# New order tables for three engines, the last store on ScalarE's queue, and split or joined small transfers in a two-layer trunk

## The chip, the cores and the metric

The kernel runs on one core of a Trainium2 chip. Its engines are TensorE (PE, matmuls), VectorE (DVE), ScalarE (ACT), GpSimd (POOL) and SyncE (SP, which here only issues transfers). Each works through its own instructions in order and waits for the others by semaphores; transfers (DMAs) are issued from the queues of SP, ACT and POOL and run on 16 DMA engines. The metric is the time of one execution on the device in microseconds (us), the median of several runs.

## What is computed

A trunk of two layers on 256 positions of 1024 columns, in 32-bit floats. Each layer has a token mixer beside a cross-attention into 256 memory tokens, an output projection, a layer norm, a SwiGLU network and another layer norm:

```python
for i in range(2):
    if i == 0:   # mixer A: gated MLP, causal in chunks of 128 positions
        u, v, q_mem = jnp.split(x @ a_w_in, [768, 1536], axis=-1)
        mix = gelu(u) * (tril(w_s) @ layer_norm(gelu(v), ln_v_g, ln_v_b) + b_s)
    else:        # mixer B: causal attention, 12 heads of 64 (256 positions are one block)
        q, k, v, q_mem = jnp.split(x @ b_w_in, [768, 1536, 2304], axis=-1)
        mix = causal_attention(q, k, v)
    sub = jnp.concatenate([mix, memory_cross_attention(q_mem, mem, w_mem_kv[i])], -1) @ w_mix_out[i]
    x = layer_norm(ALPHA * x + sub, ln_mix_g[i], ln_mix_b[i])
    g, h = jnp.split(x @ w_ffn_in[i], 2, axis=-1)
    x = layer_norm(ALPHA * x + (silu(g) * h) @ w_ffn_out[i], ln_ffn_g[i], ln_ffn_b[i])
```

The sums with b_s are over groups of 64 columns, with one bias for each group and position.

## The kernel before

*Splits.* Every operand of a matmul is written as a high part and a low part, and a product is three passes (high-high, high-low, low-high). The high part is a cast on ScalarE (L376), the low part a subtraction on VectorE (L377), both by a helper, so that most of these two engines' work carries those two lines. Names that begin with spl_ are such pairs of a weight; x0T, x1T, x2T and x3T are the pairs of the transposed activations ahead of each projection or FFN.

*Weights.* They lie in main memory as units of 1 MB or less and are loaded ahead by SyncE (L237) into four raw buffers and, for one unit of each FFN group, into one of two buffers (gb, vbig) which also hold vectors of the layer norms. Each unit is split in two halves, _0 and _1, in ten buffers. A raw buffer comes free when VectorE has split its second half; SyncE's next load then goes out. In the FFN, pairs of column blocks (groups s..1, 3, 5, 7, 9) are computed by seven products M1 to M7 of combined blocks in place of eight. The combined weights are formed by additions on VectorE (L255) or by accumulating transfers, which GpSimd issues (L219) as soon as the M1 or M3 half in the same buffer has been split.

*Order.* TensorE runs in the order in which the program is written. For VectorE, ScalarE and SyncE, three tables of numbers (VECTOR_ORDER, SCALAR_ORDER, SYNC_ORDER) say in which order the instructions of each engine stand, by their number in the program; `keep_order` (L354 and after) chains them so. GpSimd has no table.

*Places that matter below.* The start: v's projection (va) from x0T. At 24 to 60 us: SyncE loads memory tokens (mraw), the gate's weights (wsT) and position biases (bs, L928, into the ends of the buffers named wsT and vn), the norm's vectors gv, and the units vm0, o0_0 to o0_3; the memory attention's scores (sm) need key tiles that ScalarE and VectorE write through one pair of buffers (kkm, L639 and L640; klm, L641). At 100 to 146 us the first FFN begins: for each group, products Xf, Yf, Zf in PSUM are added up in m1f, m5f and u2f; m5f times the sigmoid sgf (L801) is transposed by TensorE (tpf, L822) for the FFN's second matrix. At 262 to 285 us the FFN's norm: residual with the mixer norm's gain and offset (gain_rows, L531 and L532), statistics (L483, L489), L491 adds the epsilon, GpSimd takes the power -1/2 (L492), then L495 (minus mean, times gain) and L496 (times the power, plus offset), and TensorE transposes the result (ptb). At 300 to 355 us the second mixer's scores (s) from qks, at 372 to 395 us the second FFN's start (x3T, m1g, transposes ptc). At the end the last norm works on pieces of 512, 384 and 128 columns and stores each (L498).

## Time and profile before

| what | us |
|---|---|
| three runs of the kernel before | 564.76, 565.12 (median), 566.11 |
| profiled execution, its own time | 564.97 |
| its span, first to last instruction | 563.2 |
| TensorE's matmuls begin / end | 1.05 / 555.4 |
| last VectorE instruction ends | 559.4 |
| last store issued | 559.96 |

The span is what the trace covers; the other 1.8 us lie around it. All times below are counted from the span's start. TensorE's clock was granted at 0.994 of its full speed. The page's lines and the views are shown where the prediction uses them. A waits row tells which instruction waited for which, for how long in total, how often, and the longest; a timeline row gives start, duration, engine, line, operation, output<-inputs, count, and in brackets the idle time ahead of it with what ended it.

### The profile page before, as it was taken

How to read it: one execution, taken by the hardware profiler on the slowest of the kernel's cores; microseconds unless marked ns; L12 is line 12 of the kernel's file. 1: busy time of each engine (PE TensorE's matmuls, PEld its weight loads, DVE VectorE, ACT ScalarE, POOL GpSimd, SP SyncE). 2: the span in 40 equal slices, each digit the busy share in tenths (PEclk: the TensorE clock that was granted, in tenths of full speed). 3: DMA queues.
4: the chain of work that ended last, by engine and by line, in shares of the span. 5: the costliest groups of instructions: out<-in, count | busy, mean ns of one | idle time of the engine just before them, and what ended most of it. 6: DMA issues, size and time to landing. Idle time of an engine off the chain costs nothing.

```text
span 563.2 us, 8144 instructions
## 1 busy us (share of the span) xinstructions
PE 550.1 (98%) x3035; PEld 473.9 (84%) x3035; DVE 503.2 (89%) x697; ACT 389.5 (69%) x605; POOL 49.7 (9%) x61
## 2 busy tenths in 40 slices
PE   8999999999999999999999999999999999999994
PEld 8999879888788888888899989787888888888884
DVE  6898958699999999999997988579999999999985
ACT  5767749865877867685466998667868684857710
POOL 1020012020201020100100000101202020201000
PEclk9999999999999999999999999999999999999997
DMA  8999927238887789688278335422869987897502
GB/s 315 407 348 358 356 81 219 76 59 220 246 262 245 184 310 288 213 259 296 111 285 314 129 124 197 88 101 112 184 222 185 377 168 288 181 328 168 216 0 76
DMA packets 23336, 121.01 MB, mean 215 GB/s; under 512 B 2688, under 2 KB 4992, under 8 KB 12928
## 3 DMA queue, kind: packets, MB, share of 16 engines
q1 hardware_dynamic: 16960, 98.90, 46.1%
q0 software_dynamic: 5760, 20.97, 20.8%
q10 hardware_dynamic: 576, 0.61, 0.3%
q8 instruction: 24, 0.39, 0.3%
q14 instruction: 16, 0.13, 0.1%
HBM read 119.42 MB, written 1.05 MB: 214 GB/s over the span
## 4 chain that ended last, share of the span: by engine, by line
PE 73%; DVE 11%; DMA 6%; issue 5%; ACT 4%; POOL 1%; SPq 0%; DVEq 0%; ACTq 0%; POOLq 0%
PE Xg L401 9%; PE fog L401 9%; PE fof L401 8%; PE Xf L401 8%; PE Zg L401 7%; PE Zf L401 5%; PE qk L401 4%; PE opa L401 4%; PE bv L401 3%; PE pvm L401 2%; PE opc L401 2%; DMA raw_s_T<-in_w 2%; DVE spl_s_M L377 2%; DMA raw_qm<-in_w 2%; DMA raw_o<-in_w 2%
## 5 line engine op out<-in xcount | busy, mean ns | idle before, releaser
L376 ACT CAST spl_s_M<-raw_s_T 128x1024 fp32r<-128x1024 f32 x80 | 82.7, 1053 | 37.3 <-DVE raw_s_T L255 34.8
L377 DVE TENSOR_TENSOR spl_s_M<-raw_s_T,spl_s_M 128x1024 fp32r<-128x1024 f32 x80 | 96.0, 1219 | 8.3 <-ACT spl_s_M L376 7.9
L377 DVE TENSOR_TENSOR spl_s_M<-raw_s,spl_s_M 128x1024 fp32r<-128x1024 f32 x60 | 71.6, 1219 | 2.3 <-ACT spl_s_M L376 2.1
L376 ACT CAST spl_s_M<-raw_s 128x1024 fp32r<-128x1024 f32 x60 | 60.7, 1053 | 12.5 <-DMA raw_s<-in_w 7.4
L401 PE MATMUL fof<-spl_w,htf 128*128 128x512 f32 x264 | 63.0, 390 | 0.0
L401 PEld LDWEIGHTS fof<-spl_w,htf 128*128 128x128 f32 x264 | 49.3, 188 | 10.2
L401 PE MATMUL fog<-spl_w,htg 128*128 128x512 f32 x228 | 54.2, 390 | 0.0
L377 DVE TENSOR_TENSOR spl_w<-raw_w,spl_w 128x1024 fp32r<-128x1024 f32 x44 | 53.0, 1216 | 0.0
L401 PEld LDWEIGHTS fog<-spl_w,htg 128*128 128x128 f32 x228 | 42.7, 188 | 8.8
L255 DVE TENSOR_TENSOR raw_s_T<-raw_s_T,raw_s 128x1024 f32<-128x1024 f32 x40 | 48.4, 1216 | 0.0
L376 ACT CAST spl_w<-raw_w 128x1024 fp32r<-128x1024 f32 x44 | 45.1, 1051 | 0.0
L219 POOL DMA_DIRECT2D raw_s<-in_w x20 | 17.2, 858 | 225.9 <-DVE spl_s_M L377 196.3
L401 PE MATMUL qk<-x2T,spl_qk 128*128 128x256 f32 x288 | 36.6, 284 | 0.0
L401 PEld LDWEIGHTS qk<-x2T,spl_qk 128*128 128x128 f32 x288 | 35.2, 191 | 0.6 <-issue 0.6
L401 PE MATMUL Xg<-spl_s_M,x3T 128*128 128x512 f32 x120 | 29.3, 391 | 0.6 <-DVE x3T L377 0.6
L401 PE MATMUL Xf<-spl_s_M,SfM 128*128 128x512 f32 x120 | 29.4, 393 | 0.0
L401 PE MATMUL Xg<-spl_s_M,SgM 128*128 128x512 f32 x120 | 29.3, 393 | 0.0
L401 PE MATMUL Xf<-spl_s_M,x1T 128*128 128x512 f32 x120 | 29.1, 391 | 0.1
L401 PE MATMUL Zf<-spl_s_M,SfM 128*128 128x512 f32 x120 | 29.0, 391 | 0.0
L401 PE MATMUL Zg<-spl_s_M,SgM 128*128 128x512 f32 x120 | 28.8, 389 | 0.0
L401 PEld LDWEIGHTS Xg<-spl_s_M,x3T 128*128 128x128 f32 x120 | 22.4, 188 | 6.1 <-DVE x3T L377 1.0
L401 PEld LDWEIGHTS Xf<-spl_s_M,x1T 128*128 128x128 f32 x120 | 22.4, 188 | 5.3 <-issue 0.5
(264 smaller groups left out, 1096.9 us busy)
## 6 DMA issues: line engine op xcount, KB each, us to landing
raw_w<-in_w SPq DMA_DIRECT2D x22, 1024.0 KB, 7.3
raw_s<-in_w SPq DMA_DIRECT2D x20, 1024.0 KB, 6.9
raw_s_T<-in_w SPq DMA_DIRECT2D x10, 1024.0 KB, 4.9
raw_s_T<-in_w POOLq DMA_DIRECT2D x20, 512.0 KB, 9.3
raw_s<-in_w POOLq DMA_DIRECT2D x20, 512.0 KB, 5.6
raw_o<-in_w SPq DMA_DIRECT2D x8, 1024.0 KB, 7.0
raw_qk<-in_w SPq DMA_DIRECT2D x6, 1024.0 KB, 4.9
raw_v<-in_w SPq DMA_DIRECT2D x7, 512.0 KB, 7.9
```

Source lines behind the costliest of these rows:

```text
L219: self.nc.gpsimd.dma_start(self.raw[name][:, sl], self.unit_ap(other)[:, sl], accum_op=ALU.add)
L255: self.nc.vector.tensor_add(raw, raw, self.raw[used[1]][:, sl])
L376: nc.scalar.copy(hi, src)
L377: nc.vector.tensor_sub(lo, src, hi.bitcast(F32))
L401: nc.tensor.matmul(o, lhsT, rhs, start=start, stop=stop, skip_group_check=on)
```

## The change

Four edits. (1) The three tables are replaced by others; VectorE and ScalarE execute the same instructions as before. (2) Of each tile's three last stores, the first two now go out on SyncE's queue and only the last, of 128 columns, on ScalarE's; before, the first and the third were on SyncE's and the second on ScalarE's. (3) Gain and offset of the FFN's norm come as two transfers of 512 KB instead of one of 1 MB, as those of the mixer's norm already did. (4) The position biases come by four transfers (two of four groups, two of two groups) instead of six of two groups. SyncE's number of instructions in its table stays 116: two fewer by (4), two more by (3). (TensorE's and GpSimd's instructions and their order are as before.) Since three lines are gone, the same code stands three lines further up behind L540: L801 becomes L798, L785 becomes L782.

```diff
 VECTOR_ORDER = (
-    0, 1, 2, 4, 3, 5, 6, 7, 9, 8, 10, 11, 12, 13, 14, 15, 16, 17, 18, 20, 19, 22, 21, 23, 24, 33, 34, 29, 35, 36, 39,
+    0, 2, 3, 4, 1, 5, 6, 7, 8, 10, 11, 9, 12, 13, 14, 16, 15, 17, 18, 19, 22, 20, 23, 21, 24, 29, 34, 33, 36, 35, 32,
...
                     if store:
-                        (nc.scalar if i % 2 else nc.sync).dma_start(out[tt * P:(tt + 1) * P, sl], r[:, sl])
+                        (nc.scalar if i == len(LAST_PIECES) - 1 else nc.sync).dma_start(out[tt * P:(tt + 1) * P, sl], r[:, sl])
...
             t = actp.tile([P, 2, D], F32, tag=tag, name=f"gb{l}{which}")
-            if which == "ffn":
-                nc.sync.dma_start(t, bcast_row(ins["ln_ffn"][l, :], 2 * D).rearrange("p (a c) -> p a c", a=2))
-            else:
-                for i, b in enumerate(("g", "b")):
-                    nc.sync.dma_start(t[:, i, :], bcast_row(ins[f"ln_mix_{b}"][l, :], D))
+            for i, b in enumerate(("g", "b")):
+                nc.sync.dma_start(t[:, i, :], bcast_row(ins[f"ln_{which}_{b}"][l, :], D))
             return t
...
-        for i in range(3):
+        for t, c, g0, g1 in ((wbig, 12 * P, 0, 4), (vbig, 12 * P, 4, 6)):
             for j in range(2):
-                nc.sync.dma_start(bsB[i][j * HD:(j + 1) * HD], ins["bs"][j:j + 1, 2 * i:2 * i + 2, :].to_broadcast([HD, 2, P]))
+                nc.sync.dma_start(t[j * HD:(j + 1) * HD, c:c + (g1 - g0) * P].rearrange("p (g t) -> p g t", t=P),
+                                  ins["bs"][j:j + 1, g0:g1, :].to_broadcast([HD, g1 - g0, P]))
...
-        "ln_ffn": np.concatenate([inp["ln_ffn_g"], inp["ln_ffn_b"]], axis=1),
+        "ln_ffn_g": inp["ln_ffn_g"], "ln_ffn_b": inp["ln_ffn_b"],
```

SyncE's queue in the first layer, from the gate's weights to the last unit of the output projection, before (a name's last number is a buffer's):

```order
L920 DMA wsT_319<-in_wsT 128x1536
L908 DMA gv_308<-in_a_ln_v 128x2x768
L237 DMA raw_vm0_416<-in_w 128x2048
L928 DMA wsT_319<-in_bs 64x256 x2
L928 DMA vn_318<-in_bs 64x256
L237 DMA raw_o0_0_475<-in_w 128x2048
L928 DMA vn_318<-in_bs 64x256
L928 DMA wsT_319<-in_bs 64x256 x2
L237 DMA raw_o0_1_534<-in_w 128x2048
L237 DMA raw_o0_2_607<-in_w 128x2048
L237 DMA raw_o0_3_745<-in_w 128x2048
```

and in the changed kernel:

```order
L237 DMA raw_km0_306<-in_w 128x2048
L917 DMA wsT_319<-in_wsT 128x1536
L909 DMA mraw3_316<-in_memT 128x2x256
L237 DMA raw_vm0_414<-in_w 128x2048
L925 DMA vn_318<-in_bs 64x256
L905 DMA gv_308<-in_a_ln_v 128x2x768
L925 DMA vn_318<-in_bs 64x256
L237 DMA raw_o0_0_473<-in_w 128x2048
L237 DMA raw_o0_1_532<-in_w 128x2048
L925 DMA wsT_319<-in_bs 64x512
L237 DMA raw_o0_2_605<-in_w 128x2048
L237 DMA raw_o0_3_743<-in_w 128x2048
```

One bias transfer (of wsT, 64x512) now stands ahead of this piece, before km0; gv goes behind vm0; the second o unit follows the first directly, where two bias rows with three transfers stood between.

VectorE in the first FFN, around the sigmoid's product m5f1 (L801), which TensorE's transposes wait for, before:

```order
L255 TENSOR_TENSOR raw_s0_3_T_1251<-raw_s0_3_T_1251,raw_s0_3_22_1348 128x1024
L793 SCALAR_TENSOR_TENSOR m1f1_1273<-m1f1_1273,u2f1_1416 128x512
L255 TENSOR_TENSOR raw_s0_3_T_1251<-raw_s0_3_T_1251,raw_s0_3_22_1348 128x1024
L377 TENSOR_TENSOR spl_s0_3_M6_0_1585<-raw_s0_3_T_1251,spl_s0_3_M6_0_1585 128x1024
L377 TENSOR_TENSOR spl_s0_3_M6_1_1595<-raw_s0_3_T_1251,spl_s0_3_M6_1_1595 128x1024
L801 SCALAR_TENSOR_TENSOR m5f1_1386<-m5f1_1386,sgf1_1544 128x512
L377 TENSOR_TENSOR spl_s0_3_M3_0_1606<-raw_s0_3_22_1348,spl_s0_3_M3_0_1606 128x1024
L377 TENSOR_TENSOR spl_s0_3_M3_1_1616<-raw_s0_3_22_1348,spl_s0_3_M3_1_1616 128x1024
```

and now (L798 is the same instruction):

```order
L255 TENSOR_TENSOR raw_s0_3_T_1249<-raw_s0_3_T_1249,raw_s0_3_22_1346 128x1024 x2
L788 TENSOR_TENSOR u2f1_1414<-u2f1_1414,Zf1_1365 128x512
L377 TENSOR_TENSOR spl_s0_3_M6_0_1583<-raw_s0_3_T_1249,spl_s0_3_M6_0_1583 128x1024
L790 SCALAR_TENSOR_TENSOR m1f1_1271<-m1f1_1271,u2f1_1414 128x512
L798 SCALAR_TENSOR_TENSOR m5f1_1384<-m5f1_1384,sgf1_1542 128x512
L377 TENSOR_TENSOR spl_s0_3_M3_0_1604<-raw_s0_3_22_1346,spl_s0_3_M3_0_1604 128x1024
L377 TENSOR_TENSOR spl_s0_3_M3_1_1614<-raw_s0_3_22_1346,spl_s0_3_M3_1_1614 128x1024
L377 TENSOR_TENSOR spl_s0_3_M6_1_1593<-raw_s0_3_T_1249,spl_s0_3_M6_1_1593 128x1024
```

The second M6 half is now split behind the product and both M3 halves. Further up, at about 122 us, the first half of group 3's M1, spl_s0_3_M1_0, stood ahead of the second; now it stands behind the second, SfM71's split, the addition m1f1 and one L255 addition.

VectorE at the start of the second FFN, around the addition m1g1 (L785) that reads the product Yg1 out of PSUM, before:

```order
L505 TENSOR_SCALAR rsc1_3806<-mvc1_3805 128x1
L377 TENSOR_TENSOR spl_s1_1_M5_1_3996<-raw_s1_1_T_3816,spl_s1_1_M5_1_3996 128x1024
L507 SCALAR_TENSOR_TENSOR ofc1_3807<-mvc1_3805,rsc1_3806 128x1
L377 TENSOR_TENSOR spl_s1_1_M6_0_4016<-raw_s1_1_T_3816,spl_s1_1_M6_0_4016 128x1024
L255 TENSOR_TENSOR raw_s1_1_T_3816<-raw_s1_1_T_3816,raw_s1_1_22_3824 128x1024
L785 TENSOR_TENSOR m1g1_3848<-m1g1_3848,Yg1_3860 128x512
L255 TENSOR_TENSOR raw_s1_1_T_3816<-raw_s1_1_T_3816,raw_s1_1_21_3820 128x1024
L377 TENSOR_TENSOR spl_s1_1_M6_1_4026<-raw_s1_1_T_3816,spl_s1_1_M6_1_4026 128x1024
L255 TENSOR_TENSOR raw_s1_1_T_3816<-raw_s1_1_T_3816,raw_s1_1_21_3820 128x1024
L377 TENSOR_TENSOR x3T_3763<-Ac10_3897,x3T_3763 128x4x128
```

and now (L782 is the same instruction):

```order
L505 TENSOR_SCALAR rsc1_3805<-mvc1_3804 128x1
L507 SCALAR_TENSOR_TENSOR ofc1_3806<-mvc1_3804,rsc1_3805 128x1
L782 TENSOR_TENSOR m1g1_3847<-m1g1_3847,Yg1_3859 128x512
L377 TENSOR_TENSOR spl_s1_1_M6_0_4015<-raw_s1_1_T_3815,spl_s1_1_M6_0_4015 128x1024
L377 TENSOR_TENSOR spl_s1_1_M5_1_3995<-raw_s1_1_T_3815,spl_s1_1_M5_1_3995 128x1024
L255 TENSOR_TENSOR raw_s1_1_T_3815<-raw_s1_1_T_3815,raw_s1_1_21_3819 128x1024
L377 TENSOR_TENSOR x3T_3762<-Ac10_3896,x3T_3762 128x4x128
L255 TENSOR_TENSOR raw_s1_1_T_3815<-raw_s1_1_T_3815,raw_s1_1_22_3823 128x1024
```

The addition has passed three instructions of a half each, and between L505 and the x3T subtraction on Ac10 there are three instructions of a whole half now, where there were six. A little ahead of this piece, the x3T subtraction on Ac00 now stands between the two L477 additions of opc10 and opc11, where it stood behind both. In the first layer's norm (272 us) the order behind the statistics was L531, L495, L491, L495, L532, L496, L496; it is now L532, L491, L495, L495, L496, L496. On SyncE, the two halves of gb0ffn stand behind the last bv unit (bv3), where the one transfer stood ahead of bv1. On ScalarE, the cast of spl_o1_0_0 stood between the two qks pairs of qk11 (L639, L640) and now stands behind both. At the end, VectorE's order of pieces was 128, 384, 512 columns in L495 and 384, 512, 128 in L496; it is now 512, 384 in L495, then in L496, then 128 in both.

114 rows, old and new, of tables (SCALAR_ORDER, SYNC_ORDER, VECTOR_ORDER) are left out of this document.

## Prediction

> **What bounds the kernel now.** I read the page's first part, then the waits of TensorE, then the stretches in which VectorE is full. All numbers are of the profiled execution (564.97 us, of which 563.2 are the span and 1.77 lie around it; the median of the runs is 0.15 above it).
>
> ```profile
> span 563.2 us, 8144 instructions
> PE 550.1 (98%) x3035; PEld 473.9 (84%) x3035; DVE 503.2 (89%) x697; ACT 389.5 (69%) x605; POOL 49.7 (9%) x61
> ```
>
> The matmuls are busy for 550.1 of 563.2 us, and the change touches none of them. What it can win is therefore only time in which TensorE stands still. Which moments these are, the view of TensorE's waits tells (what waits, on whom, us in total, times, longest):
>
> ```profile
> PE warmup L412 <- DVE mhalf L409: 1.1, 1, 1.1
> PE Xg L401 <- DVE x3T L377: 0.6, 1, 0.6
> PE tpf L822 <- DVE m5f L801: 0.6, 1, 0.6
> PE ptc L515 <- DVE m1g L785: 0.5, 1, 0.5
> PE sm L401 <- DVE klm L641: 0.4, 1, 0.4
> PE ptb L515 <- DVE xres L496: 0.4, 1, 0.4
> PE s L401 <- ACT qks L640: 0.4, 1, 0.4
> PE va L401 <- DVE x0T L442: 0.3, 1, 0.3
> PE sm L401 <- ACT kkm L640: 0.3, 1, 0.3
> PE va L401 <- ACT spl_v L376: 0.3, 1, 0.3
> PE pg L401 <- DVE x3T L377: 0.2, 1, 0.2
> ```
>
> The warm-up at the start stays. The other ten add up to 4.0 us, each happens once, and none is on a transfer directly: VectorE or ScalarE does something else first. The bound is TensorE's own work plus ten badly placed instructions plus the tail. An order table can cure such a place, but it pays with what it pushes back. How much room there is for that, the stretches show (length; busy time of PE, PEld, DVE, ACT, POOL, each with its count; clock, DMA share, GB/s):
>
> ```profile
> 100.00:145.00 45.00, 44.60 (x206) 36.33 (x204) 39.73 (x46) 31.59 (x49) 3.44 (x4) 1.00 0.53 151
> 145.00:260.00 115.00, 114.72 (x524) 95.39 (x525) 111.50 (x111) 84.48 (x104) 11.96 (x14) 1.00 0.82 248
> ```
>
> From 145 to 260 us VectorE is busy for 111.5 of 115 us. A delay that enters there has 3.5 us of idle time in which to be made good.
>
> **Part by part.** *The position biases and o's units (24 to 60 us).*
>
> ```profile
> 24.77 2.96 SPq L928 DMA_DIRECT2D wsT<-in_bs  x2
> ...
> 38.51 8.08 SPq L237 DMA_DIRECT2D raw_o<-in_w  x3
> ```
> ```profile
> 48.42 1.05 ACT L376 CAST spl_o<-raw_o 128x1024 fp32r<-128x1024 f32 x1 [0.50 <-DMA raw_o<-in_w]
> ```
>
> In SyncE's and ScalarE's timelines (start, us), the first two bias transfers hold SyncE's queue for 2.96 us, three further ones stand between o's first unit and its second, which goes out at 38.51, and ScalarE waits at 48.42 for the third unit before it can come to the memory scores' casts. Now there are four transfers; the second unit follows the first at once. I take it that this moves the casts ahead of TensorE's need and removes both `sm` waits: 0.4 + 0.3 = **-0.7**. Bounds: nothing, if the units land no earlier because the transfers ahead of them fill the engines anyway; and +0.5, if the start goes wrong. There the subtraction for x0T moves ahead of the first split (the `va` wait of 0.3 goes), but later ones move behind splits of other units. I cost the start at nothing: what it gains or loses is taken up at the `sm` matmuls as long as anything waits there, and counts in full once nothing does.
>
> *M5's gate (145 us).* VectorE's timeline, the chain that ended last, and the transfer view of 120 to 136.5 us (its digits are the busy share of the 16 DMA engines in 40 slices of 0.41 us; its second row is the accumulating transfers, issued by GpSimd):
>
> ```profile
> 142.14 2.49 DVE L377 TENSOR_TENSOR spl_s_M<-raw_s_T,spl_s_M 128x1024 fp32r<-128x1024 f32 x2
> 144.54 0.68 DVE L801 SCALAR_TENSOR_TENSOR m5f<-m5f,sgf 128x512 f32<-128x512 f32 x1
> ```
> ```profile
> 125.41 10.33 DMA raw_s_T<-in_w
> ```
> ```profile
> DMA  0000095799999999999999998999999952220090
> ...
> q0 software_dynamic: 576, 2.10, 71.3%
> ```
>
> The second of the two splits now comes after the gate, so the gate is ready 2.49 / 2 = 1.2 us earlier, and the wait of 0.6 goes. Against it: one M1 half is now split only after the other half (1.2), a smaller split and a PSUM addition (0.7 each, as the gate) and an operand addition (1.2), together 3.8, less 0.1 of overlap each: 3.5 us later. GpSimd's last two accumulating transfers wait for it, and M5's splits wait for them (they landed at 125.41 + 10.33 = 135.74). The digits show the engines full from about 122 to 133.6 us, 2.10 MB in 11.6 us. Half of that (1.05 MB) takes 5.8 us. With the last issue at 128.9 the first pair of transfers is then nearly through; the second runs from about 128.7, since its first half goes out a little ahead, to 134.5 instead of 133.6, and lands 0.9 later. This uses up the 0.6 us (1.2 - 0.6) that the gate had to spare and leaves a wait of 0.3: **-0.3**. Bounds: -0.6 with landing as before; +2.3 with all of the 3.5 us (0.6 - 1.2 + 3.5 = 2.9 in place of 0.6).
>
> *Layer norm of the first layer (272 us).*
>
> ```profile
> 269.42 0.75 DVE L495 SCALAR_TENSOR_TENSOR xres<-xres,mvf,gb0ffn 128x512 f32<-128x512 f32 x1
> 270.08 0.15 DVE L491 TENSOR_SCALAR rsf<-mvf 128x1 f32<-128x1 f32 x1
> 270.14 0.75 DVE L495 SCALAR_TENSOR_TENSOR xres<-xres,mvf,gb0ffn 128x512 f32<-128x512 f32 x1
> 270.81 0.69 DVE L532 TENSOR_TENSOR xres<-xres,gb0mix 128x512 f32<-128x512 f32 x1
> 271.95 1.41 DVE L496 SCALAR_TENSOR_TENSOR xres<-xres,rsf,gb0ffn 128x512 f32<-128x512 f32 x2 [0.46 <-POOL rsf L492]
> ```
>
> L491 starts GpSimd's power, and L496 waits 0.46 for it. In the new table one L532 stands ahead of L491 where an L531 and an L495 stood: 0.6 earlier, so L496 starts 0.5 earlier and the `ptb` wait goes: **-0.4**. The gain and offset rows now come as two halves, issued behind the last bv unit, and L495 needs the gain rows at 269.42 or a little later:
>
> ```profile
> 260.20 0.33 SPq L237 DMA_DIRECT2D raw_bv<-in_w  x1
> ```
> ```profile
> DMA to landing us min/median/max: 7.3/7.7/8.1
> ```
>
> The second row is of gb0mix, which already came in two such halves. The gain half goes out last, at about 260.20 + 2 x 0.33 = 260.9 (the issue time of the bv row), and lands by 269.0 at the slowest of them: half a us to spare, so nothing is added; without that cover each us late is one of TensorE. Bounds -0.4 and 0.
>
> *Scores of the second layer (320 us).*
>
> ```profile
> 318.82 1.06 ACT L376 CAST spl_o<-raw_o 128x1024 fp32r<-128x1024 f32 x1
> 319.89 0.37 ACT L639 CAST qks<-qk 64x256 fp32r<-64x256 f32 x1
> 320.27 0.37 ACT L640 CAST qks<-qk 64x256 fp32r<-64x256 f32 x1
> ```
>
> The cast of o's half (1.06 us) no longer stands ahead of the second qks pair, for which TensorE waited 0.4: **-0.4** (bounds -0.4 and 0).
>
> *Into the second FFN (380 to 394 us).*
>
> ```profile
> 379.42 1.42 DVE L477 SCALAR_TENSOR_TENSOR xres<-xres,opc 128x512 f32<-128x512 f32 x2
> 380.76 0.68 DVE L377 TENSOR_TENSOR x3T<-Ac,x3T 128x512 fp32r<-128x512 f32 x1
> ...
> 389.57 0.68 DVE L785 TENSOR_TENSOR m1g<-m1g,Yg 128x512 f32<-128x512 f32 x1
> ```
>
> One of the two L477 goes behind x3T's subtraction, which is ready 0.7 earlier: the 0.6 goes. The `m1g` addition, which frees the bank that `ptc` waits for, moves ahead of two splits and an operand addition, but cannot start before its product Yg is complete, so I take 0.3 of its 0.5. The later x3T half passes one operand addition: 0.2. Together **-1.1** (bounds -1.3, and 0 if the M5 and M6 halves, now later, are missed in turn).
>
> *The tail.*
>
> ```profile
> 559.20 1.09 SPq L498 DMA_DIRECT2D out<-xres  x2
> ```
>
> The last two stores go out from one queue, the second 1.09 - 0.33 = 0.76 after the first. VectorE's work behind the last matmul is the same in sum, but the smallest piece, now on ScalarE's queue, waits for no other issue: **-0.4** (bounds -0.76 and 0). [...]
>
> Sum: -0.7 - 0.3 - 0.4 - 0.4 - 1.1 - 0.4 = -3.3; 564.97 - 3.3 = 561.7 us, in which the 0.15 to the median is left aside.
>
> **The rivals.** (1) *The waits move.* Speaks for it: VectorE is busy 111.5 of 115 us behind 145, so what passes ahead there delays a split that TensorE soon needs, and the ten waits are so short (0.2 to 0.6) that a shift of half a split makes another. Against it: most edits bring forward what was late by less than one instruction. If two thirds come back as new waits, -3.3 becomes -1.1: 563.9. (2) *Slower, by the accumulating transfers.* Place: the M1 half of group 3. If these transfers take their 10.33 us however late they start, M5's splits come 3.5 later, the gate costs +2.3 in place of -0.3, and with 3.5 us of idle time to 260 VectorE carries a good part of it to the next products, another 2.5 or so: 564.97 - 3.0 + 2.3 + 2.5 = 566.8. It decides from a landing at about 137, and outweighs the rest from about 139 on. (3) *The tables do nothing that TensorE sees:* the waits stand because a producer that the rows do not name is late as well; only the tail's 0.4 remains: 564.6.
>
> **How the numbers follow.** Forecast 0.64 (alone 559.2 to 563.2), rival 1 0.18, rival 2 0.12, rival 3 0.06. The least time takes all ten waits (4.0), the tail's 0.76 and about 0.1 for TensorE's refilling after each wait, my choice: -5.8, 559.2. The upper end takes in rivals 1 and 3: 565.0; what lies out is rival 2. A measurement of this kernel tells 0.3% (1.7 us) from no change; below 563.4 is faster: 0.64, within it rivals 1 and 3: 0.24, slower: rival 2, 0.12.
>
> **What would show it.** In the waits of TensorE the rows of `tpf`, `Xg`, `ptb`, `s`, `sm` should be gone or below 0.2, the second o unit issued before 36 us, M5's half landed before 137, L491 ahead of L495, and the last store's issue within 0.2 us of VectorE's last instruction. The forecast is wrong if new rows of 0.5 us or more stand in the waits between 145 and 175 us or at 390, if L495 waits for gb0ffn, or if the start's `va` rows grow past 1 us while `sm` waits for nothing.

## The result and the profile after

| | kernel before | changed kernel |
|---|---|---|
| median, us (runs) | 565.24 (6) | 561.26 (6) |
| profiled execution, us | 564.97 | 561.61 |
| its span, us | 563.2 | 559.9 |

The changed kernel takes 0.9926 of the time of before (95% interval 0.9913 to 0.9938), 4.0 us less by the medians; 561.7 had been predicted. The profiled execution of the changed kernel is the slowest of its six; the two profiles differ by 3.28 us in span. Medians and intervals are those of fast runs; one slow execution of e10_best2 below (1949.7 us) is left out. The page's first lines and TensorE's waits of the changed kernel:

```profile
span 559.9 us, 8132 instructions
PE 549.4 (98%) x3035; PEld 475.6 (85%) x3035; DVE 504.6 (90%) x697; ACT 388.1 (69%) x605; POOL 48.4 (9%) x61
```
```profile
PE warmup L412 <- DVE warm L407: 1.1, 1, 1.1
PE pt L1060 <- DVE mix L377: 0.7, 1, 0.7
PE sm L401 <- ACT kkm L637: 0.5, 2, 0.3
PE opa L401 <- DVE mix L377: 0.4, 1, 0.4
PE va L401 <- DVE x0T L442: 0.3, 1, 0.3
```

The matmuls take what they took. Of the ten waits `Xg`, `tpf`, `ptc`, `ptb`, `s` and `pg` are gone. One `va` row stays, the `sm` waits stand under another producer (0.5 us in place of 0.7, though the stretch is no shorter, as the table shows), and `opa` and `pt` are new. So the balance is of gains and losses. Where they arise is read best from the starts of the matmuls: TensorE's order is the same in all these kernels, so each of the 3035 matmuls can be set beside the same one of before. Each column is a stretch between two matmuls, named by what waits in it, with the times in the profile of before; a number says by how many us the stretch became longer (+) or shorter. "Tail" is what lies behind the last matmul's start; the last column is the whole span.

| kernel | 1-43 start | 43-67 `sm` | 67-71 `opa` | 71-142 | 142-149 `tpf` | 149-293 `ptb` | 293-339 `s` | 339-355 `pt` | 355-401 `Xg`, `ptc`, `pg` | 401-555 | tail | span |
|---|---|---|---|---|---|---|---|---|---|---|---|---|
| changed | +0.61 | +0.47 | +0.76 | -0.84 | -0.77 | -1.29 | -0.81 | +0.89 | -1.87 | +0.02 | -0.45 | -3.28 |
| e1_head_old | +0.60 | -0.26 | 0.00 | -0.77 | -0.55 | -1.25 | -0.82 | +0.88 | -1.87 | +0.02 | -0.03 | -4.05 |
| e4_pt | +1.52 | +0.23 | +0.75 | -0.84 | -0.77 | -1.28 | -0.82 | +0.31 | -1.85 | +0.07 | -0.48 | -3.17 |
| e6_best | +0.41 | +0.50 | 0.00 | -0.82 | -0.77 | -1.29 | -0.82 | +0.33 | -1.85 | +0.04 | -0.05 | -4.33 |
| e7_m1_late | +0.65 | -0.23 | +0.77 | +5.56 | -0.66 | -1.31 | -0.82 | +0.89 | -1.87 | +0.06 | -0.46 | +2.58 |
| e10_best2 | +0.13 | -0.25 | 0.00 | -0.28 | -0.43 | -0.71 | -0.83 | +0.33 | -1.85 | +0.13 | -0.01 | -3.77 |
| e2_head_new | +0.48 | +0.01 | +0.74 | +0.25 | +0.01 | +0.01 | -0.01 | 0.00 | -0.01 | +0.02 | -0.61 | +0.88 |
| e3_tail | +0.26 | -0.07 | 0.00 | +0.31 | -0.01 | +0.03 | -0.03 | 0.00 | -0.03 | +0.02 | -0.51 | -0.02 |
| e5_transfers | +2.07 | -0.73 | 0.00 | -0.39 | -0.33 | +0.07 | +0.01 | 0.00 | -0.03 | 0.00 | -0.64 | +0.03 |
| e8_rsf | +0.27 | -0.31 | 0.00 | +0.01 | +0.01 | -0.33 | +0.01 | 0.00 | -0.03 | -0.01 | 0.00 | -0.38 |
| e9_ffn2 | +0.11 | +2.31 | 0.00 | +0.21 | -0.01 | +0.02 | -0.01 | 0.00 | -1.77 | +7.31 | -0.18 | +8.00 |
| e11_gate | +0.03 | -0.11 | 0.00 | -0.43 | -0.77 | +0.02 | 0.00 | 0.00 | -0.04 | +0.02 | -0.15 | -1.43 |
| e12_accum | +1.91 | -0.31 | 0.00 | +0.44 | -0.59 | +0.11 | 0.00 | 0.00 | -0.02 | -0.01 | +0.01 | +1.54 |

The rows below the changed kernel are the experiments, told further down; those from e2_head_new on are built on the kernel before. They show how far a number can be trusted. Where an edit is shared, the columns from `ptb` to 401 mostly agree within 0.1 us, and where nothing is edited they read 0 within 0.1. The start, `sm` and the stretch to 142 move by 0.4 us and more with nothing edited there (the start by 1.91 in e12_accum, `sm` by 2.31 in e9_ffn2). At `tpf` a TensorE that comes later waits less: e5_transfers, 0.95 us late at 142, reads -0.33 there with nothing edited; e11_gate, 0.51 us early, has the full -0.77. The tail is looked at below. In the changed kernel's row, then, the gains from 142 to 339 us and from 355 to 401 and the losses at `opa` and `pt` belong to the order; the 0.61 of the start doesn't need to.

The two large losses at the start, in e12_accum and e5_transfers, are slower matmuls and no wait. From 5 to 8 us in the profile of before and in that of e5_transfers (columns as in the prediction's stretches; the first with a count is TensorE's):

```profile
5.00:8.00 3.00, 2.69 (x13) 2.18 (x14) 2.46 (x7) 1.44 (x3) 0.00 (x0) 1.00 1.03 406
```
```profile
5.00:8.00 3.00, 2.74 (x9) 2.13 (x8) 2.54 (x7) 1.83 (x4) 0.00 (x0) 1.00 1.00 400
```

TensorE is as busy, but 9 matmuls pass and not 13. This view gives the clock as 1.00 in both, yet the trace has its first record of the full clock at 4.0 us in the profile of before, at 10.3 in e5_transfers and 10.1 in e12_accum, and at 4.2 to 7.0 in the others. So when TensorE gets its full clock at the start differs from execution to execution; what decides it is not known here.

**Why the head loses.** SyncE's timeline of the changed kernel, SyncE's waits from 8 to 62 us, and VectorE's timeline:

```profile
29.81 5.39 SPq L237 DMA_DIRECT2D raw_o<-in_w  x2
...
41.17 0.34 SPq L237 DMA_DIRECT2D raw_o<-in_w  x1
```
```profile
SPq L237 <- DVE spl_km L377: 4.5, 1, 4.5
```
```profile
34.73 2.57 DVE L377 TENSOR_TENSOR spl_km<-raw_km,spl_km 128x1024 fp32r<-128x1024 f32 x1
...
39.90 1.21 DVE L377 TENSOR_TENSOR spl_km<-raw_km,spl_km 128x1024 fp32r<-128x1024 f32 x1
...
47.88 8.03 DVE L377 TENSOR_TENSOR spl_o<-raw_o,spl_o 128x1024 fp32r<-128x1024 f32 x7
55.94 0.42 DVE L638 TENSOR_TENSOR klm<-hkm,kkm 64x256 fp32r<-64x256 f32 x1
```

The second o unit does go out ahead of 36 us, at 34.9. But the third finds no free raw buffer: it waits 4.5 us for the split of km0's second half (39.90 to 41.1; in the profile of before that split ran from 35.54), and goes out at 41.17, 2.2 us later than before. VectorE is late there: it has waited 1.4 us for a cast of memT, and km0's first split took 2.57 us in place of 1.23. Behind that VectorE splits seven o halves in one piece, without a gap; only then, at 55.94, comes the first klm, which before came at 54.55. At `sm` the wait for the last klm goes (0.48 us won by the starts), and matmuls just ahead of it lose more than that (0.95 here, 0.48 in e2_head_new). The `opa` wait is of the same kind; VectorE's and TensorE's timelines:

```profile
69.15 0.42 DVE L377 TENSOR_TENSOR mix<-gt,mix 128x256 fp32r<-128x256 f32 x1
```
```profile
69.63 1.21 PE L401 MATMUL opa<-spl_o,mix 128*128 128x512 f32 x4 [0.44 <-DVE mix L377]
```

The last subtraction for mix now stands behind scalings (L566) of the memory attention, at 69.15; before it began at about 64.3.

**Why 339 us loses.** VectorE's and TensorE's timelines of the changed kernel:

```profile
336.66 1.23 DVE L377 TENSOR_TENSOR spl_o<-raw_o,spl_o 128x1024 fp32r<-128x1024 f32 x1
337.92 0.42 DVE L377 TENSOR_TENSOR mix<-pv,mix 128x256 fp32r<-128x256 f32 x1
```
```profile
338.40 0.55 PE L1060 MATMUL pt<-ident,pb 128*128 128x128 f32 x3 [0.66 <-DVE mix L377]
```

A whole o half stands ahead of a small subtraction on which TensorE's transposes wait 0.66 us. The prediction did not look at this place, because nothing waited there before.

### The profile page after: what moved, and what is told of

It reads as the page before. It is cut to its first block, busy times and chain, and to the rows that moved or that the text cites. A ratio compares the mean times of both kernels' runs of the same rounds, so it can differ in the third digit from the quotient of the medians.

```text
span 559.9 us, 8132 instructions
## 1 busy us (share of the span) xinstructions
PE 549.4 (98%) x3035; PEld 475.6 (85%) x3035; DVE 504.6 (90%) x697; ACT 388.1 (69%) x605; POOL 48.4 (9%) x61
## 4 chain that ended last, share of the span: by engine, by line
PE 84%; DMA 6%; DVE 5%; issue 2%; ACT 2%; SPq 0%; POOLq 0%; POOL 0%; ACTq 0%; DVEq 0%
PE fof L401 11%; PE Xg L401 10%; PE Xf L401 10%; PE fog L401 9%; PE Zf L401 7%; PE Zg L401 7%; PE qk L401 6%; PE opc L401 4%; PE opa L401 3%; PE bv L401 3%; DMA raw_o<-in_w 2%; PE pg L401 2%; PE pf L401 2%; DMA raw_qm<-in_w 2%; PE pvm L401 2%
## 5 line engine op out<-in xcount | busy, mean ns | idle before, releaser
L401 PEld LDWEIGHTS fof<-spl_w,htf 128*128 128x128 f32 x264 | 49.4, 188 | 10.1
L255 DVE TENSOR_TENSOR raw_s_T<-raw_s_T,raw_s 128x1024 f32<-128x1024 f32 x40 | 48.3, 1220 | 0.2
L219 POOL DMA_DIRECT2D raw_s_T<-in_w x20 | 17.3, 865 | 108.9 <-DVE mb L551 74.7
```

The source lines that it names most:

```text
L219: self.nc.gpsimd.dma_start(self.raw[name][:, sl], self.unit_ap(other)[:, sl], accum_op=ALU.add)
L255: self.nc.vector.tensor_add(raw, raw, self.raw[used[1]][:, sl])
L401: nc.tensor.matmul(o, lhsT, rhs, start=start, stop=stop, skip_group_check=on)
```

## The experiments

"Before" and "changed" in a table's edit are the tables of those kernels. In the expectations "the changed kernel" and "before" mean the same. Names in the diffs below lack the digits that follow a letter: spl_s_3_M_0_1585 is the half spl_s0_3_M6_0.

| kernel | us, median (runs) | ratio to before, 95% interval |
|---|---|---|
| e1_head_old | 560.24 (4) | 0.9910 (0.9896 to 0.9925) |
| e2_head_new | 565.77 (11) | 1.0007 (0.9998 to 1.0017) |
| e3_tail | 564.57 (12) | 0.9984 (0.9970 to 0.9998) |
| e4_pt | 561.81 (5) | 0.9936 (0.9921 to 0.9951) |
| e5_transfers | 565.12 (10) | 1.0014 (0.9997 to 1.0031) |
| e6_best | 562.14 (6) | 0.9947 (0.9928 to 0.9966) |
| e7_m1_late | 568.88 (5) | 1.0078 (1.0049 to 1.0108) |
| e10_best2 | 561.10 (5) | 0.9928 (0.9915 to 0.9941) |
| e8_rsf, e9_ffn2, e11_gate, e12_accum | 564.51, 573.0, 563.46, 566.43 (1 each) | |

### The head, taken out and put in alone

e1_head_old, from the changed kernel:

```diff
-VECTOR_ORDER = changed
+VECTOR_ORDER = before[:99] + changed[99:]
-SCALAR_ORDER = changed
+SCALAR_ORDER = before[:86] + changed[86:]
-SYNC_ORDER = changed        # four bias transfers
+SYNC_ORDER = before[:40] + changed[38:]        # six bias transfers
```

> The changed kernel, but with the tables and the six bias transfers of before for the first 75 us (up to the mixer's last splits); everything behind as changed. Theory A: the new head costs TensorE 1.8 us by 75 us, and the changed first FFN has room, so the matmuls come earlier again and only what the M5 gate holds at 145 us (ready about 0.7 us before it is needed now) is lost: a wait of about 1 us there, total 560.2 to 560.5. Rival B: the gate's time is set by the accumulating transfers alone, the head's loss was time that TensorE would have waited there anyway: 561.2, no change, with waits of about 1.5 us between 138 and 146 us. Rival C: the head's loss is a true loss: 559.4.

Measured: 560.24 us. The `opa` loss is gone from the table. The time is that of theory A, but not for its reason: no wait comes back at `tpf`. The transposes there start as much earlier as in the changed kernel, and only 0.20 us is lost again, at 148.4.

e2_head_new, from the kernel before, is the opposite edit:

```diff
-VECTOR_ORDER = before
+VECTOR_ORDER = changed[:99] + before[99:]
-SCALAR_ORDER = before
+SCALAR_ORDER = changed[:86] + before[86:]
-SYNC_ORDER = before        # six bias transfers
+SYNC_ORDER = changed[:38] + before[40:]        # four bias transfers
```

> The kernel before, but with the changed tables and the four bias transfers for the first 75 us; everything behind, the stores and the 1 MB gain transfer as before. Theory A: TensorE is 1.8 us late at 75 us, and the two waits of before at 139 and 145 us (about 1.1 us together) are taken up by it: 565.9. Rival: the whole chain moves with it: 567.0. Other rival: the head is not what costs, and the total stays at 565.2.

Measured: ratio 1.0007, so no gain; in its profile 0.74 are lost at `opa` and nothing is won at `sm`. The time lies at theory A's 565.9, but the waits that were to take up the loss are still there (`tpf` 0.5 us). What follows: the new head wins nothing, in either surrounding, and loses 0.74 to 0.77 us at `opa` in all four profiles that have it (changed, e2, e4, e7). As a time this loss stays within what the runs can tell: the interval of e1_head_old overlaps that of the changed kernel.

e5_transfers has SyncE's part of e2_head_new alone; VectorE and ScalarE stand as before:

```diff
-SYNC_ORDER = before        # six bias transfers
+SYNC_ORDER = changed[:38] + before[40:]        # four bias transfers
```

> The kernel before with SyncE's changed order up to 75 us and the four bias transfers, VectorE and ScalarE as before. Theory A: the merged and moved transfers win nothing by themselves: o's second unit goes out some 3 us earlier, but its third and fourth wait for a raw buffer that VectorE frees by its splits of km0 and vm0, at 39 and 46 us as before; the sm waits of 0.7 us stay, 565.3. Rival B, as predicted: the units land earlier and both sm waits go: 564.6. Rival C: the changed queue order is itself what makes the changed head late: 566 or more.

Measured: ratio 1.0014 with 1 inside its interval (0.9997 to 1.0031); the 0.7 us of rival B, a ratio of 0.9988, lies outside. This fits the theory that the transfers were not what the `sm` matmuls waited for. Its profile shows -0.73 at `sm`, but its start had lost 2.07 us, and a TensorE that comes later waits less; so the profile alone decides nothing here.

### The tail

e3_tail, from the kernel before:

```diff
-(nc.scalar if i % 2 else nc.sync).dma_start(out[tt * P:(tt + 1) * P, sl], r[:, sl])
+(nc.scalar if i == len(LAST_PIECES) - 1 else nc.sync).dma_start(out[tt * P:(tt + 1) * P, sl], r[:, sl])
...
-VECTOR_ORDER = before
+VECTOR_ORDER = before[:662] + changed[662:]
```

> The kernel before with the changed stores and the changed order of the last tile's last normalisation alone. Forecast's term: 0.4 us less, 564.8, last store issued right behind VectorE's last instruction. [...] Rival: the last landing is set by the 512-column store, no change, 565.2.

Measured: ratio 0.9984 (0.9970 to 0.9998). The last rows of ScalarE's queue and of VectorE in the changed kernel:

```profile
556.76 0.35 ACTq L498 DMA_DIRECT2D out<-xres  x1
```
```profile
556.38 0.35 DVE L496 SCALAR_TENSOR_TENSOR xres<-xres,rsg,gb1ffn 128x128 f32<-128x128 f32 x1
```

The last store is issued 0.03 us behind VectorE's last instruction; before it was 0.52 (559.96 against 559.44). VectorE's work behind the last matmul's start has become 0.12 longer (4.41 against 4.29), so the last issue comes 0.36 us earlier by that matmul (4.45 in place of 4.81; in e3_tail also 4.45). That is about one issue time (0.35 us in ScalarE's row above). So the mechanism is seen, and its size in time is only known to lie between 0.1 and 1.7 us by the interval.

Two things in the other profiles limit it. In e2_head_new and e5_transfers, which have the old stores but two transfers fewer in SyncE's table (114 in place of 116), the last store goes out 4.49 and 4.50 us behind the last matmul's start: there, by these starts, the new stores would win only 0.05 (an estimate). And the time from the last issue to the end of the span goes with that number in all 14 profiles: 2.90 to 2.93 us with 114 transfers, 3.05 to 3.23 with 116, 3.54 to 3.58 with 118 (e1_head_old, e6_best, e10_best2). These two add up to the tail column: e5_transfers, with the old stores, is 0.64 shorter (0.31 and 0.33), and e10_best2, with the new, only 0.01 (0.37 won, 0.35 lost). How the number of transfers comes to matter at the end no run shows.

### The gate at 145 us and the accumulating transfers

e11_gate, from the kernel before, VectorE's rows:

```diff
 L377 TENSOR_TENSOR spl_s_3_M_0_1585<-raw_s_3_T,spl_s_3_M_0_1585 128x1024
+L801 SCALAR_TENSOR_TENSOR m5f_1386<-m5f_1386,sgf_1544 128x512
 L377 TENSOR_TENSOR spl_s_3_M_1_1595<-raw_s_3_T,spl_s_3_M_1_1595 128x1024
-L801 SCALAR_TENSOR_TENSOR m5f_1386<-m5f_1386,sgf_1544 128x512
```

> The kernel before, with one instruction moved: the product with the sigmoid (L801) ahead of the split of the second M6 half. Theory A: the wait of 0.6 us ahead of the transposes at 145 us goes, and matmul by matmul TensorE is 0.5 to 0.6 us earlier from there; nothing is given back by 175 us. Rival B (the M6 half is missed in turn, VectorE being busy 111.5 of 115 us): a new wait of 0.3 us or more between 146 and 175 us.

Measured: -0.77 at `tpf`, the whole of what the changed kernel gains there, with one instruction moved, and nothing given back. That is more than the 0.56 of the waits row. TensorE's timeline of before shows why:

```profile
145.28 0.33 PE L822 MATMUL tpf<-ident,m5f 128*128 128x128 f32 x1 [0.56 <-DVE m5f L801]
145.45 0.27 PE L822 MATMUL tpf<-ident,m1f 128*128 128x128 f32 x1
145.56 0.27 PE L822 MATMUL tpf<-ident,m5f 128*128 128x128 f32 x1
```

A transpose lasts 0.27 us, but where nothing waits the next starts 0.11 behind it (145.45 and 145.56). The wait is counted from the end of the record before, so it leaves out 0.27 - 0.11 = 0.16; and the first start behind the wait comes 0.17 in place of 0.11 later (145.28 and 145.45). 0.56 + 0.16 + 0.06 = 0.78. The waits of the weight loads, which start ahead of their matmuls (by 0.22 us in the median of the 3035 in the profile of before), tell the same from the other side. Their rows in the profile of before, for the six matmuls whose waits the change removed:

```profile
PEld ptb L515 <- DVE xres L496: 1.1, 2, 0.8
...
PEld Xg L401 <- DVE x3T L377: 1.0, 1, 1.0
PEld tpf L822 <- DVE m5f L801: 0.9, 1, 0.9
PEld ptc L515 <- issue: 0.7, 1, 0.7
...
PEld pg L401 <- DVE x3T L377: 0.6, 1, 0.6
...
PEld s L401 <- ACT qks L640: 0.6, 1, 0.6
```

These six add up to 4.9 us where the matmuls' rows have 2.7 (0.4 + 0.6 + 0.6 + 0.5 + 0.2 + 0.4). By the starts, the changed kernel gains 3.7 at these six places (0.62 at `ptb`, 0.60 at `Xg`, 0.78 at `tpf`, 0.62 at `ptc`, 0.48 at `pg`, 0.62 at `s`). So the matmul's row was a bound from below at each, and the weight load's one from above, but for `s`, which gained 0.06 more. The other 1.0 of the 4.74 in the four columns was won at matmuls that had no row: 0.65 at further transposes of the layer norm, 0.19 at scores of 312 us, 0.10 at one `Xg`, and small change.

e12_accum adds to e11_gate the late M1 half:

```diff
-L377 TENSOR_TENSOR spl_s_3_M_0_1441<-raw_s_3_T,spl_s_3_M_0_1441 128x1024
 L377 TENSOR_TENSOR spl_s_3_M_1_1451<-raw_s_3_T,spl_s_3_M_1_1451 128x1024
 L377 TENSOR_TENSOR htf_1393<-tpf_1388,htf_1393 128x512
 L377 TENSOR_TENSOR SfM_1237<-Aa_1175,SfM_1236 128x512
 L255 TENSOR_TENSOR raw_s_1_T<-raw_s_1_T,raw_s_1_21_1245 128x1024
+L377 TENSOR_TENSOR spl_s_3_M_0_1441<-raw_s_3_T,spl_s_3_M_0_1441 128x1024
```

> As e11_gate, and with the first half of M1 of group 3 split some 3.8 us later, behind an operand addition, as in the changed kernel, so that GpSimd's accumulating transfer for it goes out about 3 us later. Theory A (the 16 DMA engines are full until 133 us whichever transfer goes first, so the transfer lands no later than before): as e11_gate at 145 us, 0.5 to 0.6 us earlier than before. The prediction's working (lands 0.9 later): 0.3 earlier. The prediction's second rival (each transfer takes its 10.3 us however late it starts): M5's split starts at about 139 us in place of 136, and TensorE is 2.3 us later than before at 145 us.

Measured: -0.59 at `tpf`, +0.44 in the stretch to 142. GpSimd's timeline, and the transfer view's row of these two transfers (KB each, median us from issue to landing):

```profile
125.97 0.85 POOL L219 DMA_DIRECT2D raw_s_T<-in_w  x1 [1.48 <-issue]
129.12 0.86 POOL L219 DMA_DIRECT2D raw_s_T<-in_w  x1 [2.30 <-DVE spl_s_M L377]
```
```profile
raw_s_T<-in_w POOLq DMA_DIRECT2D x2, 512.0 KB, 7.3
```

The late transfer is issued 3.15 us behind its partner (1.14 before) and lands at 136.35, after 7.2 us, where the last one of before took 10.33. So the prediction's second rival, in which a transfer keeps its 10.33 us and the gate costs 2.3, is refuted at this place. Nor does the late issue delay the landing: in e11_gate the first of the four transfers goes out at 120.47 and the last lands at 134.87; in e12_accum, an execution that is late from its start, these are 122.15 and 136.35, so 1.68 and 1.48 later. For the landing theory A holds, and not the 0.9 of the prediction's working. The `tpf` column doesn't decide it, since TensorE comes 2.0 us late to 142; and the +0.44 lies at one product that waits for m5f, in a stretch that moves by -0.43 to +0.31 with nothing edited in it. In the changed kernel the landing is early too; GpSimd's rows:

```profile
119.56 0.88 POOL L219 DMA_DIRECT2D raw_s<-in_w  x1 [23.95 <-DVE spl_s_M L377]
...
128.53 0.86 POOL L219 DMA_DIRECT2D raw_s_T<-in_w  x1 [2.93 <-DVE spl_s_M L377]
```

Only the fourth transfer is late (3.1 us), and the first goes out 1.0 us ahead of the 120.54 of before although TensorE was 1.9 us behind at 99 us: the queue of transfers starts earlier and has less left when the late one comes (at 128.53 the queue has moved 1.36 MB of the 2.10 of the four; in the profile of before it was 1.16). It takes 5.7 us and lands at 134.2, where the last one of before landed at 135.7.

e7_m1_late, from the changed kernel, puts the same split behind four more halves:

```diff
-L377 TENSOR_TENSOR spl_s_3_M_0_1439<-raw_s_3_T,spl_s_3_M_0_1439 128x1024
 L255 TENSOR_TENSOR raw_s_1_T<-raw_s_1_T,raw_s_1_21_1243 128x1024
...
 L377 TENSOR_TENSOR spl_w_0_1_1499<-raw_w_0_1314,spl_w_0_1_1499 128x1024
+L377 TENSOR_TENSOR spl_s_3_M_0_1439<-raw_s_3_T,spl_s_3_M_0_1439 128x1024
```

> The changed kernel with VectorE's split of the first M1 half of group 3 a further five instructions later, so that GpSimd's last accumulating transfer goes out at about 133 us instead of 128.5. Theory A: up to 128.5 the lateness was free because the 16 engines were full with the earlier ones until 133; beyond that each us counts: landing near 138.5, M5's splits 3 us late, the gate at 146.5, TensorE waits about 1 us at 145 us and loses perhaps 1 more behind it: 562.3 to 563.3. Rival B: VectorE's and ScalarE's room there takes it up: 561.3. Rival C, the prediction's slower rival in full: 4.5 us late and little made good: 565.

Measured: 568.88 us, which none of the theories gave, and for another reason than theirs. TensorE's waits, and three stretches of 4 us (length, TensorE's busy time and count, granted clock, DMA share, GB/s):

```profile
PE Xf L401 <- DVE spl_s_M L377: 4.6, 1, 4.6
```
```profile
130.00:134.00 4.00, 0.00 (x0) 0.99 0.00 0
134.00:138.00 4.00, 3.83 (x10) 0.58 0.45 65
138.00:142.00 4.00, 4.00 (x19) 1.00 1.02 335
```

The product Xf needs this very half and waits 4.6 us for it; behind that TensorE is 6.7 us late, which alone can explain that the gate's wait is gone (-0.66). The run says that the half has little room left ahead of its own product, and nothing on what a late transfer costs at the gate.

### The layer norm at 272 us

e8_rsf, from the kernel before:

```diff
 L489 BN_AGGR mvf_2531<-stf_2497 128x2
+L491 TENSOR_SCALAR rsf_2533<-mvf_2531 128x1
 L531 TENSOR_TENSOR xres<-xres,gb0mix 128x512
-L495 SCALAR_TENSOR_TENSOR xres<-xres,mvf_2531,gb0ffn 128x512
-L491 TENSOR_SCALAR rsf_2533<-mvf_2531 128x1
-L495 SCALAR_TENSOR_TENSOR xres<-xres,mvf_2531,gb0ffn 128x512
+L495 SCALAR_TENSOR_TENSOR xres<-xres,mvf_2531,gb0ffn 128x512 x2
```

> The kernel before with one VectorE instruction moved: L491 of the first layer's FFN norm directly behind the statistics, 1.2 us earlier. Theory: L496's wait for GpSimd's power (0.46) goes and with it TensorE's wait at ptb: the matmuls from 273 us on come 0.4 to 0.6 earlier than before, against the matmuls ahead of 270 us. Rival: the two halves of L496 are late for another reason, no step there.

Measured: -0.33, and L496 waits no more for GpSimd. So the predicted mechanism gives about 0.4, as predicted, but the changed kernel gains 1.29 there. VectorE's timeline of the changed kernel:

```profile
268.79 0.20 DVE L489 BATCH_NORM_AGGREGATE mvf<-stf 128x2 f32<-128x12 f32 x1
268.90 0.64 DVE L532 TENSOR_TENSOR xres<-xres,gb0mix 128x512 f32<-128x512 f32 x1
269.46 0.15 DVE L491 TENSOR_SCALAR rsf<-mvf 128x1 f32<-128x1 f32 x1
269.52 1.41 DVE L495 SCALAR_TENSOR_TENSOR xres<-xres,mvf,gb0ffn 128x512 f32<-128x512 f32 x2
270.85 1.41 DVE L496 SCALAR_TENSOR_TENSOR xres<-xres,rsf,gb0ffn 128x512 f32<-128x512 f32 x2
```

Between the statistics (L489) and L496 stand one addition and two L495; before, two additions and two L495, and the wait. The L531 has gone ahead of the statistics. So L496 starts 2.06 us behind L489 in place of 3.20: 1.1 earlier. What TensorE makes of it, the starts of its matmuls tell: 0.62 at the first transposes (272.8 us), which is the wait of the row with what the row leaves out; 0.25 at those of the next columns (273.5); and 0.40 at the transposes of the other 128 positions (284 us), whose L496 starts at 282.28 in place of 283.36. The last two places have no row among TensorE's waits. In e8_rsf the gain lies at the first place alone (0.38). What the L531 does alone was not tried.

### Into the second FFN (355 to 401 us)

e9_ffn2, from the kernel before, has the changed order of that place alone:

```diff
-VECTOR_ORDER = before
+VECTOR_ORDER = before[:474] + changed[474:511] + before[511:]
-SCALAR_ORDER = before
+SCALAR_ORDER = before[:416] + changed[416:451] + before[451:]
```

> The kernel before, with the changed order of VectorE and ScalarE between 379 and 408 us only. Theory A (the gain at 381 to 394 us comes from this stretch alone): matmul by matmul against the kernel before, TensorE is 1.2 to 1.8 us earlier by 395 us and stays so to the end; the waits Xg, ptc and pg are gone; span about 561.6. Rival B (the gain needs the earlier splits and loads of the whole table): at most 0.6 us. Rival C (it is given back behind 395 us, since splits of the second FFN were pushed back): earlier at 395, level with before at the last matmul.

Measured: -1.77 at the place, as in the changed kernel, and then +7.31: rival C, far above the gain. At 424.8 us Xg has waited 4.7 us for m5g. The timeline of e9_ffn2:

```profile
408.80 0.86 POOL L219 DMA_DIRECT2D raw_s_T<-in_w  x1 [0.20 <-issue]
...
410.57 0.33 SPq L237 DMA_DIRECT2D raw_w<-in_w  x1
...
418.89 1.05 ACT L376 CAST spl_s_M<-raw_s_T 128x1024 fp32r<-128x1024 f32 x1 [2.84 <-DMA raw_s_T<-in_w]
...
423.98 0.68 DVE L797 TENSOR_TENSOR m5g<-m5g,Xg 128x512 f32<-128x512 f32 x1
```

and that of the changed kernel:

```profile
405.08 0.86 POOL L219 DMA_DIRECT2D raw_s_T<-in_w  x1 [0.20 <-issue]
...
413.70 1.06 ACT L376 CAST spl_s_M<-raw_s_T 128x1024 fp32r<-128x1024 f32 x1 [0.76 <-DMA raw_s_T<-in_w]
413.73 0.33 SPq L237 DMA_DIRECT2D raw_s_T<-in_w  x1
...
414.75 0.68 DVE L794 TENSOR_TENSOR m5g<-m5g,Xg 128x512 f32<-128x512 f32 x1
415.35 1.22 DVE L377 TENSOR_TENSOR spl_s_M<-raw_s_T,spl_s_M 128x1024 fp32r<-128x1024 f32 x1
```

In e9_ffn2 the cast that the last accumulating transfer releases starts 10.1 us behind its issue (408.80 to 418.89), with unit loads of SyncE issued from 410.57 on. The addition m5g comes 5.1 us behind that, since it stands behind the split of that half, two operand additions (L255) and the addition u2g, as in the kernel before. In the changed kernel the cast starts 8.6 us behind the issue (405.08 to 413.70), SyncE's next load goes out only at 413.73, and m5g stands ahead of that half's split (415.35), so it doesn't wait for the transfer at all. So the gain at 355 to 401 is bought with later splits and accumulating transfers, and two things elsewhere in the tables stand in for it: SyncE loads the T buffer first and the other units behind it, and m5g stands between M5's two splits. Which of the two carries more was not separated.

### A better version?

e4_pt, from the changed kernel, moves the small mix pair ahead of o's halves; VectorE's and ScalarE's rows:

```diff
+L377 TENSOR_TENSOR mix_1_2823<-pv_3311,mix_1_2823 128x256
 L377 TENSOR_TENSOR spl_o_1_1_3581<-raw_o_1_3219,spl_o_1_1_3581 128x1024
-L377 TENSOR_TENSOR mix_1_2823<-pv_3311,mix_1_2823 128x256
...
+L376 CAST mix_1_2823<-pv_3311 128x256
 L376 CAST spl_o_2_0_3584<-raw_o_2_3351 128x1024
-L376 CAST mix_1_2823<-pv_3311 128x256
```

> The changed kernel with one half moved on two engines at 336 us: the mix1_1 cast ahead of the spl_o1_2_0 cast on ScalarE, and the mix1_1 subtraction ahead of the spl_o1_1_1 split on VectorE. Theory: the changed kernel's new wait of 0.7 us for the transposes pt goes and stays gone: 560.6. Rival: the next scores or transposes wait in its place within 20 us: 561.2.

Measured: the `pt` column falls from +0.89 to +0.31 and the row `pt` is gone from the waits, yet the time is 561.81: its start took 1.52 us more than that of before, against 0.61 in the changed kernel's profile.

e10_best2, from e1_head_old, is the same edit:

```diff
+L377 TENSOR_TENSOR mix_1_2825<-pv_3313,mix_1_2825 128x256
 L377 TENSOR_TENSOR spl_o_1_1_3583<-raw_o_1_3221,spl_o_1_1_3583 128x1024
-L377 TENSOR_TENSOR mix_1_2825<-pv_3313,mix_1_2825 128x256
...
+L376 CAST mix_1_2825<-pv_3313 128x256
 L376 CAST spl_o_2_0_3586<-raw_o_2_3353 128x1024
-L376 CAST mix_1_2825<-pv_3313 128x256
```

> The changed kernel with the order of before in the first 75 us, and the last split half of the second mixer moved ahead at 336 us. Theory A: the two gains add, 560.2 less the 0.6 us that the second edit gained in the trace (0.85 won at 338 us, 0.25 given back at 348): 559.4 to 559.9 us. Rival B (the second edit moves the wait and gains nothing): 560.1 to 560.6 us. Rival C (the head's loss comes from the execution and not from the order): 561 us or more.

Measured: 561.1 us, where 559.4 to 559.9 was expected. `pt` falls to +0.33 again and `opa` is 0, but the stretches from 71 to 293 gained 1.15 us less than in e1_head_old, whose order is the same there. By the starts, 0.56 of it lies at one product Xf at 138.9, which waits 0.3 us for m5f, 0.12 at 148.4, 0.37 at 162.0 and 0.10 at 171.7. TensorE had come to 71 us 0.46 earlier than in e1_head_old, so it met producers that were not ready; why these were not earlier too was not settled. The time is that of rival C.

e6_best adds to e10_best2 a move of the memory scores' casts:

```diff
+L636 CAST kkm_587<-hkm_588 64x256
+L637 CAST kkm_587<-hkm_588 64x256
 L376 CAST mix_1_672<-gt_686 128x256
 L376 CAST mix_0_671<-gt_686 128x256
-L636 CAST kkm_587<-hkm_588 64x256
-L637 CAST kkm_587<-hkm_588 64x256
...
+L638 TENSOR_TENSOR klm<-hkm_588,kkm_587 64x256
 L964 TENSOR_TENSOR gt_702<-sv_693,wsT 128x512
 L964 TENSOR_TENSOR gt_718<-sv_709,vn 128x512
-L638 TENSOR_TENSOR klm<-hkm_588,kkm_587 64x256
```

> The head of before with the rest as changed (the version that gave 560.24), plus three moves: the two mix1_1 instructions at 336 us as in the run on pt; and at 56 us the casts of the second key tile ahead of the casts of mix0 on ScalarE, and its subtraction ahead of the addition of gt1 on VectorE. Theory: the pt wait (0.7) and the two sm waits (0.6 together) go and nothing takes their place: 559.0. Rival: what is pushed back is missed at once (opa waits for mix0, or the next scores): 560.2.

Measured: 562.14 us; `sm` rose to +0.50 where e1_head_old has -0.26. Moving one key tile forward made a later one late: the `sm` matmuls wait 1.4 us for the last klm. The ratios of e1, e4, e6, e10 and the changed kernel lie between 0.991 and 0.995 and each interval overlaps that of the changed kernel, so none of these versions beats the changed kernel measurably.

## Why the prediction was right, and where it was not

The forecast (faster, 561.7 us) holds, and the sum of its terms, -3.3 us, is that of the profile, -3.28 (the medians differ by 4.0). That is partly luck: the terms for the waits were too small and those for the losses missing, by like amounts.

- **Position biases and o's units: -0.7 predicted; 0 at `sm` and +0.75 at `opa` by the order.** The step that failed is "I take it that this moves the casts ahead of TensorE's need". It followed SyncE's queue, and the second o unit did go out at 34.9; but the load behind it waits for VectorE's split of km0, and VectorE, full from 47.88 to 55.94, brings klm no earlier. e2_head_new (no gain) and e5_transfers (no gain from the transfers alone) show it. That a late mix could stop `opa` was not seen at all.
- **M5's gate: -0.3 predicted, -0.77 measured** (e11_gate: -0.77 alone, in one execution). The mechanism was right. Two sizes were off, of the terms "the wait of 0.6 goes" and "lands 0.9 later": the wait costs TensorE 0.77 and not 0.6, and the 0.9 for a later landing does not show in the changed kernel, since only one of the two halves is late and the transfers ahead go out earlier: M5's half lands at 134.2, 1.6 us earlier than before.
- **Layer norm: -0.4 predicted, -1.29 measured.** L491 stands ahead of L495, and L495 doesn't wait for gb0ffn, as predicted; e8_rsf gives that part as -0.33. The mis-sized step is "L496 starts 0.5 earlier": it starts 1.1 earlier, as an L531 more had gone from behind the statistics, which the order rows told. And the gain does not end with the `ptb` row of 0.4: 0.65 of it lies at transposes that had no row.
- **Scores of the second layer: -0.4 predicted, -0.81 measured**, alike in all six profiles with that order (-0.81 to -0.83). The `s` row explains 0.4 and what it leaves out some 0.2; the other 0.19 lies at scores of 312 us that had no row. No run has this edit alone.
- **Into the second FFN: -1.1 predicted, -1.87 measured.** Three rows of 1.3 us together, with three times 0.16 or a little more, give 1.8. The share of 0.3 for m1g was too cautious. The bound "0 if the M5 and M6 halves are missed in turn" was the right worry: e9_ffn2 pays 7.31 us where the rest of the tables does not stand in.
- **A new wait at `pt`: not predicted, +0.89.** Rival 1 (waits move) had it in kind, but the prediction looked for it between 145 and 175 us and at 390, where VectorE is full. It came where an o half was put ahead of a small instruction that TensorE waits for.
- **Tail: -0.4 predicted, -0.45 in the profile**, of which 0.36 is the store's earlier issue; the rest lies between that issue and the end of the span. The 0.76 between two issues on one queue, from which the term came, is 0.44 and 0.45 in the two kernels with two transfers fewer.
- **The lower end, 559.2.** No run shows the 0.1 of "TensorE's refilling after each wait" as a time of its own; it was the author's choice. What the starts at the gate show beyond the row's 0.56 is 0.22: 0.16 that the row leaves out and 0.06 at the second transpose.
- **Rivals.** (1) came true in part: `opa` and `pt` give back 1.65 of the 4.74 that the four places gained, a third and not two. (2) is refuted at 145 us by e12_accum, yet lateness of accumulating transfers does appear in e9_ffn2. (3) is refuted by e11_gate alone.

## What to carry to other kernels

A row in TensorE's waits understates what its cure brings: take it as a lower bound and the weight load's row as roughly an upper one (at the six matmuls here 2.7 and 4.9, with 3.7 measured). Matmuls that wait too little for a row can gain as well (1.0 here). So compare the starts of the same matmuls in two profiles, which resolves 0.1 us in most stretches where whole runs scatter by 1. An order table's gain in one place is often held up by its entries elsewhere, so a piece of it taken over alone can cost several times what it wins (-1.77, then +7.31). Before a wait is put down to a transfer, see whether the engine that must use the data, or free the buffer for the next load, has any idle time ahead of it.

## What was not expected of the hardware

**TensorE's granted clock was lower behind two long waits, and once behind several short ones.** In e7_m1_late the stretch of 4 us behind the 4.6-us wait has a granted clock of 0.58, and 10 matmuls pass and not the 19 of the next one, at 1.00. In e9_ffn2, behind the wait of 4.7 us, it is 0.50 from 424.8 to 428.5. In e9_ffn2 it was also lower from 60.5 us on, where no single wait was over 0.44 us (the columns are as in the stretches above):

```profile
58.00:60.50 2.50, 1.73 (x10) 1.00 0.38 128
60.50:64.50 4.00, 3.56 (x18) 0.60 1.01 408
```

This is where e9_ffn2 loses most of its 2.31 at `sm`, with the same order there as before. In the profile of before TensorE is busy for 1.78 us of the same 2.5, hardly more than the 1.73 here, and from 60.5 to 64.5 its clock is 1.00 and 31 matmuls pass and not 18. What decides when the clock falls was not shown.

**Some VectorE subtractions took 0.8 to 1.3 us longer beside GpSimd's work on wsT.** GpSimd's row in the timeline of the changed kernel, and then in that of before:

```profile
34.06 2.16 POOL L918 TENSOR_SCALAR_AFFINE_SELECT wsT<-wsT 128x1536 f32<-128x1536 f32 x1 [30.86 <-DMA wsT<-in_wsT]
```
```profile
33.24 1.83 POOL L921 TENSOR_SCALAR_AFFINE_SELECT wsT<-wsT 128x1536 f32<-128x1536 f32 x1 [30.03 <-DMA wsT<-in_wsT]
```

Beside the first, km0's split, begun at 34.73, took 2.57 us in place of 1.23 and ended 1.08 us after GpSimd's instruction (37.30 against 36.22). Beside the second, a subtraction for memT (0.69 elsewhere) began at 34.14, took 1.47 and ended 0.54 after GpSimd's. Both ended within 0.15 us of the time at which they would have, had they begun when GpSimd finished. But not every VectorE instruction is longer there: qqm (L632), begun at 33.69 beside the second, took its usual 0.42. Why the two are longer no run here shows, and the prediction had no term for it. Which instruction stands there goes with the order of the tables: with that of before it is the one of 0.69 us (1.47 in e1_head_old too), and with the changed one the split of km0's first half (2.57 in e2_head_new and e4_pt too), ahead of the one on which SyncE's third o unit waits.
